# Attention's value products placed one bank behind the transposes, with new spacings for the side work of a two-layer hybrid block

## The chip, the core and the metric

The kernel runs on one core of a Trainium2 chip. A core has a matrix engine, TensorE (PE in the rows, with its weight loads as PEld), and four engines beside it: VectorE (DVE), ScalarE (ACT), GpSimd (POOL) and SyncE (SP), which here issues most of the transfers. Each engine works through a queue of its own in order, and semaphores make one wait for another. The metric is the time of one execution on the device in microseconds (us); less is better.

## What is computed

Two layers, each a feed-forward, a mixer and a second feed-forward, on 256 tokens of width 1024 in float32. Cut to what matters:

```python
for l in range(2):
    x = x + 0.5 * swiglu(rms_norm(x, n1[l]), w1, w2)          # width 2816
    h = rms_norm(x, n2[l])
    u, v, rq, rk, rv, rg, q, kv, gate = split(h @ w_in[l])
    y_a = gelu(u) * (tril(ws) @ layer_norm(gelu(v)) + bs)       # gated mlp, 4 groups
    y_b = silu(rg) * group_norm(retention(rq, rk, rv))          # 4 heads
    y_c = g0 * compressed + g1 * selected + g2 * window         # attention, 8 heads
    ga, gb, gc = split(sigmoid(h @ w_merge[l] + b))
    x = x + (ga*(y_a @ wb[0]) + gb*(y_b @ wb[1]) + gc*(y_c @ wb[2])) @ w_o[l]
    x = x + 0.5 * swiglu(rms_norm(x, n3[l]), w3, w4)
return rms_norm(x, final)
```

At this length the selected and the window branch both see every earlier token, so each of the two is plain causal attention with a bias by distance; the kernel calls them the two `b` of a unit.

## The kernel before

**Weights.** Every weight matrix is cut into pieces of up to 128 x 1024 numbers. `issue` (lines 206 to 228) loads a piece, and splits it into a rounded part (`hi`, a cast on ACT, line 219) and the rest (`lo`, a subtraction on DVE and, for a share set by `pool_lo`, on POOL, line 223). There are four buffers for raw and four for split pieces, and pieces are issued up to three ahead. Activations are split in the same way, so that one product is three matmuls in the fast float32 form (`mm_feat`): high by high, high by low, low by high. Almost all matmuls go through the helper `mm` (line 147), all transposes through `transpose` (line 157).

**Order on PE.** The order of PE's instructions is the order of the program; that of the other engines is chosen by a scheduler when the program is built, by a priority that follows the order of the program. `soon()` raises the priority of what stands in it by 120 instructions. The main stream (the feed-forward's and the mixer's large products) is one generator that yields after each three matmuls. Small work with a chain of its own (attention, retention, the gated mlp, the compressed branch, the column and the transposes of a norm) stands in other generators, the sides. A counter `clk` adds an assumed duration for each matmul (0.1095 for a product of 256 columns). A side that yields a number sleeps until the counter has grown by it; one that yields a condition sleeps until an event is set. After each yield of the main stream `run_sides` goes through the sides and lets those go on that are due; what they emit stands in PE's queue at this place. The `WAIT_` constants are these numbers.

**Attention.** `attention` runs four units one after the other: query tile 0 and 1, group 0 and 1 (`unit`). A unit emits scores for four heads, `WAIT_SCORE[qt]` apart, with the softmax on DVE and ACT (lines 642 to 651); before its second head it waits until the unit before has emitted its last transposes. After `WAIT_P` it goes through its banks (two for tile 0, four for tile 1): four transposes of probabilities into a bank of tag `sc`, a split of them into `ph` (ACT, line 680) and `pl` (DVE, line 681, shown as a part of tile `xhl`), then, `WAIT_PT[qt]` later, the two products `pv` with the values into bank `o`. `cmp_branch` (two of them) does the softmax of the compressed branch, transposes it after `WAIT_CB`, multiplies it when both units of the tile are done, adds it, and splits the sum into `yh[2]` and `yl[2]` (lines 725 to 727).

**The other sides.** `retention` ends in two sets of four transposes into a bank each, which ACT reads four times (line 798). `gmlp` is there four times, once a group; all four start when retention's normalised rows and the mlp's layer norm are there, sleep `WAIT_GMLP`, and emit their products into a bank of tag `ms`, which DVE's addition (line 849) empties. PSUM has two banks `mm`, three `sc`, one `o`, two `ms`.

**Norms.** A norm's scale is applied late: `x_update` (line 376) adds a finished tile of 128 features to x, and `norm_tile` makes the next stage's split operand of it (ACT line 311, DVE line 312) and its squares (`square`: POOL lines 327 to 337; the last tile's square on ACT and its sum on DVE). The side `norm_end` sleeps, emits two short float32 products (`norm_col`: the sum over features as a column), sleeps again, and emits two transposes that spread the factor; the next stage's evacuations wait for it, not its products. The mixer's last part, the output projection, has eight such tiles, one piece each; during it splits are shared 5 to 3 between DVE and POOL.

Of the kernel before, what the change touches and what calls it, by code (L numbers as in the profile page):

```python
# [39 lines left out]
WAIT_FOLD = 3.0  # L40
WAIT_CMP = 7.0
WAIT_COPY = 0.5
WAIT_SCORE = (5.3, 4.5)
WAIT_PT = (4.5, 2.6)
WAIT_CB = 8.0
WAIT_GN = 3.5
WAIT_OB = 1.5
WAIT_LN = 6.0
WAIT_GMLP = 10.0
WAIT_VR = 3.5  # L50
WAIT_P = (2.5, 4.5, 2.5, 2.5)


def _pieces():
# [11 lines left out]
def tile_hybrid_block(  # L66
# [28 lines left out]
    def nm(s):  # L95
        uid[0] += 1
        return f"{s}_{uid[0]}"
# [34 lines left out]
    def soon():  # L132

        return tc.high_priority(offset=EARLY)
# [21 lines left out]
    def transpose(o, i):  # L156
        nc.tensor.transpose(o, i, ident)  # L157
        clk[0] += 0.109
# [17 lines left out]
    def side(gen):  # L176
        sd = Side(gen)
        sd.kind = gen.__name__
        sides.append(sd)
        return sd  # L180
# [127 lines left out]
    def norm_tile(st, k, late=False):  # L308
        if st["i"] < 6:
            g = g_norm[:, st["i"], k:k + 1]  # L310
            S.activation(st["h"][:, k], xs[k], AF.Copy, scale=g)  # L311
            V.scalar_tensor_tensor(st["l"][:, k], xs[k], g, st["h"][:, k].bitcast(F32), op0=ALU.mult, op1=ALU.subtract)  # L312
        if late:
            return
        square(st, k)
# [58 lines left out]
        return lambda: "R" in st  # L374

    def x_update(d, p, nst):
        V.scalar_tensor_tensor(xs[d], p, 0.5, xs[d], op0=ALU.mult, op1=ALU.add)  # L377
        norm_tile(nst, d)


    def ffn(st, nxt, first=False, load=None):
# [104 lines left out]
    def mixer(l, st, nxt):  # L486
# [126 lines left out]
        def unit(qt, g):  # L613
# [52 lines left out]
            def pv(n):  # L666
                b, kb = banks[n]
                ph, pl = PT.pop(n)
                v2 = VS[:, kb, b, 2 * g:2 * g + 2].rearrange("p c d -> p (c d)")
                mm(o, lhsT=v2, rhs=ph, start=n == 0, stop=False)  # L670
                mm(o, lhsT=v2, rhs=pl, start=False, stop=n == len(banks) - 1)

            for n, (b, kb) in enumerate(banks):
                pt = psc()
                for j in range(4):
                    transpose(pt[:, j * 128:j * 128 + 128], Ps[j][:, b, kb * 128:kb * 128 + 128])
                ph = act.tile([128, 512], F32R, tag="ph", name=nm("ph"), bufs=2)
                pl = PL[n % 2]
                with soon():
                    S.copy(ph, pt)  # L680
                    V.tensor_tensor(out=pl, in0=pt, in1=ph.bitcast(F32), op=ALU.subtract)
                PT[n] = (ph, pl)
                if n == len(banks) - 1:
                    ev.add(f"t{qt}{g}")
                yield WAIT_PT[qt]
                pv(n)

            own, oth = slice(64 * g, 64 * g + 64), slice(64 - 64 * g, 128 - 64 * g)
            t = t2()
# [5 lines left out]
        def cmp_branch(qt):  # L695
            yield has(f"s{qt}0", f"s{qt}1")
            sc = scs[qt]
            s3 = sc.rearrange("p (h n) -> p h n", n=16)
            mx = small(8)
            V.tensor_reduce(out=mx, in_=s3, axis=AX.X, op=ALU.max)  # L700
            V.tensor_tensor(out=s3, in0=s3, in1=mx[:, :, None].to_broadcast([128, 8, 16]), op=ALU.subtract)
            S.activation(sc, sc, AF.Exp)
            yield 2.0
            V.tensor_tensor(out=sc, in0=sc, in1=ccmp[:, 1, qt].rearrange("p j g n -> p (j g n)"), op=ALU.mult)
            sm = small(8)
            V.tensor_reduce(out=sm, in_=s3, axis=AX.X, op=ALU.add)
            V.tensor_scalar(sm, sm, 1e-30, None, op0=ALU.max)
            V.reciprocal(sm, sm)
            V.tensor_tensor(out=sm.rearrange("p (j g) -> p g j", g=2), in0=sm.rearrange("p (j g) -> p g j", g=2),
                            in1=gate[qt][:, :, 0].rearrange("p (g j) -> p g j", g=2), op=ALU.mult)  # L710
            V.tensor_tensor(out=s3, in0=s3, in1=sm[:, :, None].to_broadcast([128, 8, 16]), op=ALU.mult)
            yield WAIT_CB
            p = pms()
            transpose(p[:, 0:128], sc)
            ct = sc
            S.copy(ct, p[:, 0:128])
            yield 3.0
            yield has(f"u{qt}0", f"u{qt}1", "yalloc")
            o, p = os[qt], pms()
            for j in range(4):  # L720
                mm(p[:, j * 128:j * 128 + 128], lhsT=VC[:, j], rhs=ct, start=True, stop=True)
            qs = slice(qt * 128, qt * 128 + 128)
            o3 = o.rearrange("p (j t) -> p j t", j=4)
            with soon():
                V.tensor_tensor(out=o, in0=o, in1=p, op=ALU.add)
                S.copy(yh[2][:, :, qs], o3)  # L726
                V.tensor_tensor(out=yl[2][:, :, qs], in0=o3, in1=yh[2][:, :, qs].bitcast(F32), op=ALU.subtract)
            ev.add(f"yc{qt}")
# [11 lines left out]
        def retention():  # L740
# [47 lines left out]
            for it in range(2):  # L788
                yn = yns[:, it]
                p = pms()  # L790
                y = t2()
                ts_ = slice(it * 128, it * 128 + 128)
                for h in range(4):
                    hs = slice(h * 128, h * 128 + 128)
                    transpose(p[:, hs], yn[:, hs])
                for h in range(4):
                    hs = slice(h * 128, h * 128 + 128)
                    S.activation(y[:, hs], p[:, hs], AF.Identity, scale=gnc[:, 0, h:h + 1], bias=gnc[:, 1, h:h + 1])  # L798
                y3 = y.rearrange("p (h t) -> p h t", h=4)
                V.tensor_tensor(out=y3, in0=y3, in1=sg[:, :, ts_], op=ALU.mult)  # L800
                S.activation(yh[1][:, :, ts_], y3, AF.Copy, scale=0.5)
                V.scalar_tensor_tensor(yl[1][:, :, ts_], y3, 0.5, yh[1][:, :, ts_].bitcast(F32), op0=ALU.mult, op1=ALU.subtract)
# [38 lines left out]

        def gmlp(g, z):
            yield lambda: 0 in yh and "gv" in ev and "yn" in ev
            yield WAIT_GMLP
            q = pms()
            for n in range(2):
                mm(q[:, n * 128:n * 128 + 128], lhsT=vl[n][:, g * 128:g * 128 + 128], rhs=wt[:, g], start=True, stop=True)
            y = t2()
            V.tensor_tensor(out=y[:, 0:256].rearrange("p (n t) -> p n t", n=2), in0=q[:, 0:256].rearrange("p (n t) -> p n t", n=2),
                            in1=bsb[:, g:g + 1].to_broadcast([128, 2, 128]), op=ALU.add)  # L850
            V.scalar_tensor_tensor(y[:, 256:512], y[:, 0:256], 0.5, z, op0=ALU.mult, op1=ALU.mult)
            S.copy(yh[0][:, g], y[:, 256:512])
            V.tensor_tensor(out=yl[0][:, g], in0=y[:, 256:512], in1=yh[0][:, g].bitcast(F32), op=ALU.subtract)
            ev.add(f"ya{g}")
# [209 lines left out]
        for d in range(2, 8):  # L1064
            o = pmm()[:, 0:256]
            yield from mm_feat(o, piece(8, 128), mk, True, True)
            x_update(d, o, nst)
        side(norm_end(nst))
        return nst

    def drive(gen):
# [168 lines left out]
```

## Time and profile before

| | |
|---|---|
| median of 3 runs | 1263.14 us |
| lowest, highest | 1262.05, 1270.24 us |
| the profiled execution | 1267.7 us, its span 1265.6 us |
| TensorE, weight loads | busy 98%, 97% of the span |
| VectorE, ScalarE, GpSimd | busy 71%, 53%, 40% |
| mean granted TensorE clock | 0.989 of full speed |

The profile is of one execution. A busy share is the share of the span in which an engine had an instruction at work; matmuls are pipelined and their ends are modelled. L147 is line 147 of the kernel. The views used below: the page (busy times, and the chain of work that ended last), PE's waits (who waited for whom, how long, how often, the longest), the windows (busy time of each engine in a stretch, with the number of instructions in brackets, and the granted clock as a share of 2.4 GHz), the timeline (start, duration, instruction; in square brackets the idle time before it and what ended it), and the instructions of a line with shortest, median and longest duration. In order of time the stages are: feed-forward 0 to 196 us, mixer to 451, feed-forward to 633, and again feed-forward to 819, mixer to 1076, feed-forward to 1250.

### The profile page before, as it was taken

Reading aid. Unit: us, or ns where it says so; the run is one execution under the profiler, and the core shown is the slowest. Engines: PE = TensorE matmul, PEld = TensorE weight load, DVE = VectorE, ACT = ScalarE, POOL = GpSimd, SP = SyncE. Lnnn points to the kernel's source line nnn. Section 1 sums busy time; section 2 is a strip of 40 time slices with the busy share of each in tenths; the row PEclk is TensorE's granted clock in tenths of the full one; section 3 lists DMA queues with packets and bytes.
Section 4 is the critical chain, followed back from the end, with each engine's and each line's share of the span. In section 5 each row is a group of like instructions: output and inputs, shape, how many; then the busy total and the mean of one; then the engine's idle time right before and its main releaser. Section 6 shows DMA issues by size and latency. Waiting matters only on the chain.

```text
span 1265.6 us, 26068 instructions
## 1 busy us (share of the span) xinstructions
PE 1234.9 (98%) x10432; PEld 1222.6 (97%) x10432; DVE 900.2 (71%) x1436; ACT 666.7 (53%) x1070; POOL 504.1 (40%) x419
## 2 busy tenths in 40 slices
PE   9999999998999999999999999999999999999997
PEld 9999999997998999999999999999899989999997
DVE  6766667789875867776667665687897768677653
ACT  6544445567764544554444444465676545445442
POOL 0444231174554735452215442203645548155322
PEclk9999999999999999999999999999999989999998
DMA  8865556754554566666666655675444435556562
GB/s 279 273 185 189 181 191 197 239 161 132 169 167 125 177 186 195 193 190 194 194 189 187 189 176 188 182 238 187 150 137 165 151 129 163 194 197 191 187 195 80
DMA packets 68969, 230.67 MB, mean 182 GB/s; under 512 B 8816, under 2 KB 11504, under 8 KB 68848
## 3 DMA queue, kind: packets, MB, share of 16 engines
q1 hardware_dynamic: 68256, 227.90, 57.6%
q8 instruction: 82, 1.34, 0.4%
q0 software_dynamic: 448, 1.08, 0.3%
q14 instruction: 39, 0.32, 0.1%
q10 hardware_dynamic: 144, 0.03, 0.0%
HBM read 225.80 MB, written 1.05 MB: 179 GB/s over the span
## 4 chain that ended last, share of the span: by engine, by line
PE 83%; DVE 6%; POOL 4%; ACT 3%; issue 2%; DMA 0%; SPq 0%; POOLq 0%; DVEq 0%; ACTq 0%
PE mm L147 56%; PE sc L147 23%; DVE hl L223 2%; PE ms L147 2%; POOL hl L223 2%; ACT hl L219 1%; POOL sq L333 1%; POOL acc L337 1%; PE o L147 1%; PE sc L157 1%; ACT P L646 0%; ACT t L798 0%; DMA x<-in_x_dram 0%; DVE small L649 0%; DVE P L642 0%
## 5 line engine op out<-in xcount | busy, mean ns | idle before, releaser
L219 ACT CAST hl<-raw 128x1024 fp32r<-128x1024 f32 (+3 forms) x437 | 443.2, 1016 | 336.7 <-PE mm L147 179.3
L223 DVE TENSOR_TENSOR hl<-raw,hl 128x896 fp32r<-128x896 f32 (+6 forms) x437 | 476.8, 1093 | 198.9 <-ACT hl L219 197.9
L147 PE MATMUL mm<-xhl,hl 128*128 128x256 f32 x4440 | 541.2, 280 | 3.1 <-ACT hl L219 1.1
L223 POOL TENSOR_TENSOR hl<-raw,hl 128x128 fp32r<-128x128 f32 (+2 forms) x264 | 362.5, 1375 | 431.7 <-ACT hl L219 402.0
L147 PEld LDWEIGHTS mm<-xhl,hl 128*128 128x128 f32 x4440 | 525.8, 189 | 6.2 <-ACT hl L219 1.7
L147 PE MATMUL mm<-s,hl 128*128 128x256 f32 x2496 | 293.5, 279 | 0.0
L147 PEld LDWEIGHTS mm<-s,hl 128*128 128x128 f32 x2496 | 290.7, 188 | 0.2
L147 PE MATMUL sc<-xhl,hl 128*128 128x256 f32 x2280 | 276.7, 280 | 0.0
L147 PEld LDWEIGHTS sc<-xhl,hl 128*128 128x128 f32 x2280 | 269.8, 189 | 0.0
L399 ACT CAST s<-t 128x256 fp32r<-128x256 f32 x88 | 35.7, 406 | 118.2 <-DVE t L398 118.2
L333 POOL TENSOR_TENSOR sq<-x 128x256 f32<-128x256 f32 x36 | 28.3, 786 | 131.7 <-DVE x L377 131.7
L400 DVE TENSOR_TENSOR s<-t,s 128x256 fp32r<-128x256 f32 x88 | 38.4, 437 | 38.3 <-ACT s L399 38.3
L147 PE MATMUL mm<-hl,xhl 128*128 128x256 f32 (+1 forms) x432 | 59.1, 287 | 0.0
L398 DVE TENSOR_TENSOR t<-t,t 128x256 f32<-128x256 f32 x88 | 55.8, 635 | 0.6 <-ACT t L397 0.5
L147 PEld LDWEIGHTS mm<-hl,xhl 128*128 128x128 f32 x432 | 53.7, 189 | 2.2 <-issue 1.9
L337 POOL TENSOR_TENSOR acc<-acc,sq 128x256 f32<-128x256 f32 x36 | 51.3, 1426 | 2.8
L312 DVE SCALAR_TENSOR_TENSOR xhl<-x,gnorm,xhl 128x256 fp32r<-128x256 f32 x48 | 38.8, 817 | 5.5 <-ACT xhl L311 5.5
L646 ACT ACTIVATE P<-P,small 128x128 f32<-128x128 f32 (+1 forms) x64 | 28.9, 451 | 25.5 <-DVE small L642 24.8
L396 DVE TENSOR_TENSOR t<-sc,R 128x512 f32<-128x512 f32 x44 | 30.4, 691 | 10.8 <-PE sc L147 8.2
L397 ACT ACTIVATE t<-t 128x256 f32<-128x256 f32 x88 | 36.2, 412 | 1.4 <-DVE t L396 0.7
L396 DVE TENSOR_TENSOR t<-mm,R 128x512 f32<-128x512 f32 x41 | 28.3, 691 | 8.5 <-PE mm L147 5.9
L147 PE MATMUL sc<-s,hl 128*128 128x256 f32 x192 | 27.8, 309 | 6.3 <-ACT s L726 5.0
(179 smaller groups left out, 742.2 us busy)
## 6 DMA issues: line engine op xcount, KB each, us to landing
raw<-in_w_dram SPq DMA_DIRECT2D x389, 512.0 KB, 3.8
raw<-in_w_dram SPq DMA_DIRECT2D x32, 384.0 KB, 3.1
raw<-in_w_dram SPq DMA_DIRECT2D x4, 420.0 KB, 3.2
x<-in_x_dram SPq DMA_DIRECT2D x4, 256.0 KB, 4.8
raw<-in_w_dram SPq DMA_DIRECT2D x8, 128.0 KB, 4.6
s<-in_c_alibi_dram SPq DMA_DIRECT2D x2, 512.0 KB, 8.5
lng<-in_lnp_dram SPq DMA_DIRECT2D x2, 512.0 KB, 4.2
ks<-ks POOLq DMA_DIRECT2D x4, 256.0 KB, 4.0
```

The source lines that it names most:

```text
L147: nc.tensor.matmul(o, lhsT=lhsT, rhs=rhs, start=start, stop=stop)
L219: S.copy(hi[:, s_], raw[:, s_])
L223: e.tensor_tensor(out=lo[:, a:b], in0=raw[:, a:b], in1=hi[:, a:b].bitcast(F32), op=ALU.subtract)
L312: V.scalar_tensor_tensor(st["l"][:, k], xs[k], g, st["h"][:, k].bitcast(F32), op0=ALU.mult, op1=ALU.subtract)
L333: (V if last else G).tensor_tensor(out=q, in0=xs[k], in1=xs[k], op=ALU.mult)
L337: (V if last else G).tensor_tensor(out=st["acc"], in0=st["acc"], in1=q, op=ALU.add)
L396: V.tensor_tensor(out=t3, in0=p.rearrange("p (a b) -> p a b", a=2), in1=R2, op=ALU.mult)
L397: S.activation(u[:, 0:256], t[:, 0:256], AF.Silu)
L398: V.tensor_tensor(out=u[:, 256:512], in0=u[:, 0:256], in1=t[:, 256:512], op=ALU.mult)
L399: S.copy(h4[:, j % 4], u[:, 256:512])
L400: V.tensor_tensor(out=l4[:, j % 4], in0=u[:, 256:512], in1=h4[:, j % 4].bitcast(F32), op=ALU.subtract)
L646: S.activation(Pt[:, b, 0:nk], Pt[:, b, 0:nk], AF.Exp, scale=-1.0, bias=mx[:, b:b + 1], accum_out=sm[:, b:b + 1])
```

## The change

Attention: in a unit `pv` of a bank is emitted after the transposes of the next bank, and the last one after a last wait. The spacings change: scores of query tile 1 4.2 for 4.5, `WAIT_PT` 6.0 for 4.5 (tile 0) and 2.0 for 2.6 (tile 1), `WAIT_P` of the last unit 0.5 for 2.5, the compressed branch's transposes 6.0 for 8.0 and its next step 1.5 for 3.0. Gated mlp: group g sleeps 2.5 g longer than group 0, and its addition is `soon`. Retention: the four reads of each bank on ACT are `soon`. All norms: `x_update` with what it calls is `soon`. The norm behind a mixer: the column is emitted 5.0 instead of 3.0 behind the last tile, the transposes 3.0 instead of 1.0 behind the column. No instruction is added or taken away.

```diff
--- before.py
+++ after.py
@@ -40,15 +40,17 @@
 WAIT_FOLD = 3.0
 WAIT_CMP = 7.0
 WAIT_COPY = 0.5
-WAIT_SCORE = (5.3, 4.5)
-WAIT_PT = (4.5, 2.6)
-WAIT_CB = 8.0
+WAIT_SCORE = (5.3, 4.2)
+WAIT_PT = (6.0, 2.0)
+WAIT_CB = 6.0
 WAIT_GN = 3.5
 WAIT_OB = 1.5
 WAIT_LN = 6.0
 WAIT_GMLP = 10.0
+WAIT_GROUP = 2.5
+WAIT_LATE = 5.0
 WAIT_VR = 3.5
-WAIT_P = (2.5, 4.5, 2.5, 2.5)
+WAIT_P = (2.5, 4.5, 2.5, 0.5)
 
 
 def _pieces():
@@ -374,8 +376,9 @@
         return lambda: "R" in st
 
     def x_update(d, p, nst):
-        V.scalar_tensor_tensor(xs[d], p, 0.5, xs[d], op0=ALU.mult, op1=ALU.add)
-        norm_tile(nst, d)
+        with soon():
+            V.scalar_tensor_tensor(xs[d], p, 0.5, xs[d], op0=ALU.mult, op1=ALU.add)
+            norm_tile(nst, d)
 
 
     def ffn(st, nxt, first=False, load=None):
@@ -674,6 +677,8 @@
                 pt = psc()
                 for j in range(4):
                     transpose(pt[:, j * 128:j * 128 + 128], Ps[j][:, b, kb * 128:kb * 128 + 128])
+                if n:
+                    pv(n - 1)
                 ph = act.tile([128, 512], F32R, tag="ph", name=nm("ph"), bufs=2)
                 pl = PL[n % 2]
                 with soon():
@@ -683,7 +688,7 @@
                 if n == len(banks) - 1:
                     ev.add(f"t{qt}{g}")
                 yield WAIT_PT[qt]
-                pv(n)
+            pv(len(banks) - 1)
 
             own, oth = slice(64 * g, 64 * g + 64), slice(64 - 64 * g, 128 - 64 * g)
             t = t2()
@@ -714,7 +719,7 @@
             transpose(p[:, 0:128], sc)
             ct = sc
             S.copy(ct, p[:, 0:128])
-            yield 3.0
+            yield 1.5
             yield has(f"u{qt}0", f"u{qt}1", "yalloc")
             o, p = os[qt], pms()
             for j in range(4):
@@ -793,9 +798,10 @@
                 for h in range(4):
                     hs = slice(h * 128, h * 128 + 128)
                     transpose(p[:, hs], yn[:, hs])
-                for h in range(4):
-                    hs = slice(h * 128, h * 128 + 128)
-                    S.activation(y[:, hs], p[:, hs], AF.Identity, scale=gnc[:, 0, h:h + 1], bias=gnc[:, 1, h:h + 1])
+                with soon():
+                    for h in range(4):
+                        hs = slice(h * 128, h * 128 + 128)
+                        S.activation(y[:, hs], p[:, hs], AF.Identity, scale=gnc[:, 0, h:h + 1], bias=gnc[:, 1, h:h + 1])
                 y3 = y.rearrange("p (h t) -> p h t", h=4)
                 V.tensor_tensor(out=y3, in0=y3, in1=sg[:, :, ts_], op=ALU.mult)
                 S.activation(yh[1][:, :, ts_], y3, AF.Copy, scale=0.5)
@@ -841,13 +847,14 @@
 
         def gmlp(g, z):
             yield lambda: 0 in yh and "gv" in ev and "yn" in ev
-            yield WAIT_GMLP
+            yield WAIT_GMLP + WAIT_GROUP * g
             q = pms()
             for n in range(2):
                 mm(q[:, n * 128:n * 128 + 128], lhsT=vl[n][:, g * 128:g * 128 + 128], rhs=wt[:, g], start=True, stop=True)
             y = t2()
-            V.tensor_tensor(out=y[:, 0:256].rearrange("p (n t) -> p n t", n=2), in0=q[:, 0:256].rearrange("p (n t) -> p n t", n=2),
-                            in1=bsb[:, g:g + 1].to_broadcast([128, 2, 128]), op=ALU.add)
+            with soon():
+                V.tensor_tensor(out=y[:, 0:256].rearrange("p (n t) -> p n t", n=2), in0=q[:, 0:256].rearrange("p (n t) -> p n t", n=2),
+                                in1=bsb[:, g:g + 1].to_broadcast([128, 2, 128]), op=ALU.add)
             V.scalar_tensor_tensor(y[:, 256:512], y[:, 0:256], 0.5, z, op0=ALU.mult, op1=ALU.mult)
             S.copy(yh[0][:, g], y[:, 256:512])
             V.tensor_tensor(out=yl[0][:, g], in0=y[:, 256:512], in1=yh[0][:, g].bitcast(F32), op=ALU.subtract)
@@ -1065,7 +1072,7 @@
             o = pmm()[:, 0:256]
             yield from mm_feat(o, piece(8, 128), mk, True, True)
             x_update(d, o, nst)
-        side(norm_end(nst))
+        side(norm_end(nst, WAIT_LATE, 3.0))
         return nst
 
     def drive(gen):
```

## Rows read from the trace of the kernel before

**Rows 1.** The page: busy time by engine, and shares of the chain that ended last.

```profile
PE 1234.9 (98%) x10432; PEld 1222.6 (97%) x10432; DVE 900.2 (71%) x1436; ACT 666.7 (53%) x1070; POOL 504.1 (40%) x419
...
PE 83%; DVE 6%; POOL 4%; ACT 3%; issue 2%; DMA 0%; SPq 0%; POOLq 0%; DVEq 0%; ACTq 0%
```

**Rows 2.** PE's waits over the span: us in total, times, longest us.

```profile
PE sc L147 <- ACT s L726: 5.0, 2, 2.5
PE ms L147 <- DVE t L849: 4.1, 3, 2.8
PE ms L147 <- DVE acc L337: 3.7, 2, 1.9
PE o L147 <- ACT ph L680: 2.7, 2, 1.4
PE sc L147 <- DVE s L727: 1.3, 2, 0.7
PE o L147 <- DVE xhl L681: 1.2, 2, 0.6
```

**Rows 3.** Windows: us, then busy time (count) of PE, PEld, DVE, ACT, POOL; clock, DMA.

```profile
402.00:406.00 4.00, 4.00 (x23) 4.00 (x22) 0.37 (x1) 0.33 (x1) 0.00 (x0) 0.57 0.27 109
1023.00:1031.00 8.00, 7.35 (x37) 7.15 (x38) 2.20 (x4) 1.05 (x1) 0.97 (x1) 0.57 0.20 66
1077.00:1082.00 5.00, 4.62 (x26) 4.62 (x27) 1.30 (x4) 1.32 (x2) 0.75 (x2) 0.66 0.64 213
280.00:320.00 40.00, 34.33 (x281) 32.81 (x281) 37.49 (x96) 29.49 (x66) 18.18 (x17) 1.00 0.49 143
```

**Rows 4.** Timeline of PE, front of attention and mlp, layer 0.

```profile
294.68 0.51 PE L147 MATMUL o<-xhl 128*128 128x512 f32 x1 [0.63 <-DVE xhl L681]
...
300.58 0.71 PE L147 MATMUL ms<-wt,s 128*128 128x128 f32 x4 [2.76 <-DVE t L849]
...
304.54 1.03 PE L157 MATMUL ms<-sq,s 128*128 128x128 f32 x8
```

**Rows 5.** Timeline of DVE, then of ACT, in the same stretch.

```profile
300.11 0.42 DVE L849 TENSOR_TENSOR t<-ms,bsb 128x256 f32<-128x256 f32 x1
...
306.11 2.90 ACT L798 ACTIVATE t<-ms,gnc 128x128 f32<-128x128 f32 x8
```

**Rows 6.** Timeline of PE, then of DVE, end of attention, layer 0.

```profile
392.51 0.60 PE L157 MATMUL sc<-sq,P 128*128 128x128 f32 x4
...
396.15 1.05 PE L147 MATMUL ms<-scc,s 128*128 128x128 f32 x8
...
401.10 4.49 PE L147 MATMUL sc<-s,hl 128*128 128x256 f32 x23 [0.66 <-DVE s L727]
...
393.82 0.69 DVE L681 TENSOR_TENSOR xhl<-sc,ph 128x512 fp32r<-128x512 f32 x1 [2.09 <-ACT ph L680]
```

**Rows 7.** POOL's lines (shortest/median/longest ns) in 430 to 452 us, then the timeline.

```profile
L223 POOL TENSOR_TENSOR hl<-raw,hl x7: 986/1199/1604, 431.3 to 451.3; 128x384 fp32r<-128x384 f32 x7
...
L333 POOL TENSOR_TENSOR sq<-x x6: 792/1195/1602, 432.9 to 448.9; 128x256 f32<-128x256 f32 x6
...
L337 POOL TENSOR_TENSOR acc<-acc,sq x6: 782/802/1199, 433.7 to 450.6; 128x256 f32<-128x256 f32 x6
...
447.92 1.02 POOL L223 TENSOR_TENSOR hl<-raw,hl 128x384 fp32r<-128x384 f32 x1
...
448.92 1.86 PE L147 MATMUL sc<-xhl,hl 128*128 128x256 f32 x15
```

**Rows 8.** Windows of PE: us, busy time (products), clock, DMA share, GB/s.

```profile
60.00:160.00 100.00, 100.00 (x851) 1.00 0.59 185
460.00:560.00 100.00, 100.00 (x885) 1.00 0.66 197
650.00:750.00 100.00, 100.00 (x851) 1.00 0.63 187
1090.00:1190.00 100.00, 100.00 (x885) 1.00 0.59 192
```

## Prediction

> **What bounds the kernel now.** Read the page first: TensorE (PE) is busy for 98% of the span and is 83% of the chain that ended last [rows 1]. The products are the same before and after the change, so it can only win back time in which PE stands still or runs at half clock. PE's waits come next. Six lines there hold 18.0 us [rows 2]; what else PE idles lies at the start and the end of the run, where nothing is edited, and in waits under 0.5 us. Each of the six comes once in each layer's mixer: the attention product `pv` on its split operands `ph` and `xhl` (2.7 + 1.2 us), the gated mlp on the addition that empties its bank (4.1), the branch output on attention's split result (5.0 + 1.3), the norm's column on `acc` (3.7).
>
> Third, the granted clock. Behind most of these waits PE runs at the lower of its two levels, 1.2 instead of 2.4 GHz. A stretch of length t at mean clock c has lost t(1-c). There are five such stretches; three are alike, from 402, 453 and 917 us, and one of these stands with the two others [rows 3]: three times 4 x 0.43, then 8 x 0.43 and 5 x 0.34, so 3 x 1.7 + 3.4 + 1.7 = 10.2 us. They stand behind the waits for attention's result in both layers (402, 1023), for `acc` in both (453, 1077) and for `ph` in layer 1 (917). What the change can reach is 18.0 + 10.2 = 28 us.
>
> **End of attention** (`WAIT_SCORE`, `WAIT_PT`, `WAIT_P`, `WAIT_CB`, the 1.5, `pv` one bank behind). Side work is put into PE's order by the counter `clk`, looked at after every three products, each worth 0.1095, so in steps of 0.3285. From the last scores of the last unit to its last `pv` the waits were 2.5 and four times 2.6, which is 8 + 4 x 8 = 40 steps; they become 0.5 and four times 2.0, which is 2 + 4 x 7 = 30. A score spacing of 4.5 is 14 steps, 4.2 is 13. Against that the two units of the first query tile get 6.0 for 4.5 per bank, 19 steps for 14, which delays the second unit's scores. Followed unit by unit, counting that side work itself advances `clk`, the third unit's scores end 6 products later than before, the fourth's last scores come 9 products earlier and end 12 earlier, and with the 30 of the tail attention ends 42 products earlier. A product takes 0.113 to 0.1175 us (100 us through 885 or 851, [rows 8]). Today PE is through attention's last product at about 397.0 and needs the split result until 401.1 [rows 6], 4.1 us with 3 products to fill them. With 45 products there are 45 x 0.113 = 5.1 us: no wait. The tighter tail holds: the transposes of 392.51 have their split operand at 394.5 [rows 6], 2.0 us later; the new `pv` comes 21 products and a set of transposes behind, at least 2.4 us. Gain: 5.0 + 1.3 of waits and 1.7 + 3.4 of clock, 11.4 us. Bounds: 11.4, and about 3 if DVE or ACT answer 1.5 us later beyond the margin of 1 us in each layer, since waits of 1.3 to 2.5 us stand before the half-clock stretches (the 2.8 of the mlp in layer 0 stands before none).
>
> **Front of attention and the gated mlp.** In layer 0 PE waits for `pv` until 294.68 [rows 4]. The first unit's second transposes and `pv` move back by 1.5 on the counter, 15 products or 1.7 us, so of 2.0 us some 0.3 to 0.5 stay. The four mlp products now come 2.5 apart instead of together. Today the third waits until 300.58 for the addition that starts at 300.11 [rows 4, 5]; DVE had other work before it. Spread, they let retention's two sets of transposes (now at 304.54, behind all four, [rows 4]) in between: counted out, retention's wait ends one step of three products behind the first mlp product. There are two `ms` banks. The order becomes mlp 0, transposes, transposes, mlp 1: the second transposes wait for mlp 0's addition (0.4 us if DVE is free, 3 us if it is as late as today) and mlp 1 for the four ACT reads of the first transposes (eight take 2.90 us and began 0.5 us behind the last transpose, [rows 4, 5]). `soon` moves both forward in the queues, but DVE is busy for 37.5 of the 40 us from 280 to 320 [rows 3]: it has no room to answer at once. What stays or comes new I put at 2.2 us in each layer, between 0.6 and 4. Removed are 2.7 + 1.2 + 4.1 = 8.0 us and the 1.7 us of half clock in layer 1; kept are 8.0 + 1.7 - 4.4 = 5.3 us, between 0 and 8.5.
>
> **The late norm.** The column product goes from 3.0 to 5.0 on the counter behind the last output tile: 16 steps for 10, 18 products later, 2.0 us. That covers the 1.9 us that it waits per layer, by 0.1 to 0.2. `x_update` under `soon` moves a tile's update, scaled copies, square and sum ahead of weight splits that wait. On POOL this matters: through the whole output projection POOL stands still for hardly a moment. By the medians a split there takes 1.20, a square 1.20, a sum 0.80 us [rows 7], 3.20 a tile, while PE needs 24 products, 2.7 to 2.8. POOL falls behind, and the split that ends at 448.94 is taken by PE at 448.92 [rows 7]: no cover at all. If the last tile's square and sum (2.0 us) go before that split, PE waits 2.0 us there instead. I take it that they don't: tile and split already alternate, and a split is ready before the next tile is finished. Gain: 3.7 - 0.3 of waits and 1.7 + 1.7 of clock, 6.8 us; other bound 0.
>
> At their shortest the three take 0.99 + 0.79 + 0.78 = 2.56 us [rows 7]; at that pace POOL would keep up with PE, either order would do and the 6.8 us would be safe, while at the medians and with the other order they are 0. The Trainium skill (GPSIMD Engine Reference, section 1, Specifications) says that POOL shares its SBUF interfaces with VectorE and contends with DVE instructions that have two SBUF inputs, as the weight splits and scaled copies are. By this rule bringing DVE's share of the update forward can keep POOL at the long durations; the spread of the rows agrees with it, but no row says which neighbour made which instruction long.
>
> **Edits at nothing.** `x_update` in the four feed-forwards: four weight buffers, up to three pieces split ahead, cover it, about 8 us; the update's 0.4 us on DVE and 2.0 on POOL fit. Without that cover each of 32 updates would cost up to 2. The power 3.0 instead of 1.0 behind the column: the first evacuation waits 2 us longer, with five banks to fill at 5.4 us each. Transposes ahead of `pv`: they need a third `sc` bank while scores hold two; it is free once the bank before is split, 2 us after its transposes, the same 2.4 us as above.
>
> **Sum.** 11.4 + 5.3 + 6.8 = 23.5 us. The profiled execution took 1267.7 us (span 1265.6 and 2.1 around it): 1244.2. It lies 4.6 above the median of 1263.14 and inside the runs' 1262.05 to 1270.24. On the median the sum gives 1239.6.
>
> **A term of the other sign.** PE's products run at one of two spacings at full clock: [rows 8] has 100 us of each of the four feed-forwards, with the same instructions: both first ones run at the wider spacing (851), both second ones at the closer (885). The second ones begin behind a norm that PE waited for, the first ones behind one it did not wait for. If the late norm no longer stops PE, they may start at the wider one: 0.0045 us x about 1,500 products = 6.8 us each. In layer 0 I expect the next stage to flip the other way, as the second feed-forward now does to it; layer 1 has no next stage. Both feed-forwards behind an unwaited norm being wide, I count one such stage: 1239.6 + 6.8 = 1246. That is the forecast.
>
> **Rivals.** (a) POOL's order turns against PE: the 6.8 us of the norm are not won. 1253 with the wide stage, 1246 without. For it: no cover at 448.9; against: the alternation. (b) DVE sets the pace of the front: it is 94% busy there, so waits return at the `ms` banks as in the upper bound, 5.3 us are lost: 1251 with the wide stage, 1245 without. (c) The change does not do what it says: the stalls are DVE's and ACT's backlog, and wherever PE's order puts the reader, it waits: only a third of the 23.5 is won, 1255, with the wide stage 1262. Against it: at the end of attention DVE itself idles 2.09 us for ACT, which waits for PE [rows 6]. (d) Slower: the priority puts every update's POOL work (2.0 us) before the split that PE needs next. In the output projection, six tiles a layer without cover, that is up to 6 x 2.0 us, 24 in both layers, against at most 16.7 won elsewhere: 1263.1 + 24 - 16.7 = 1270, and with a wide stage 1277. It decides from a wait of 1.4 us a tile. Against it: POOL's backlog then feeds back into a slower PE, which gives POOL time.
>
> **How the numbers follow.** The forecast's case, all three gains within their bounds and none to two wide stages, 0.50, 1237 to 1252. (a) 0.16, (b) 0.14, (c) 0.12, (d) 0.08. Range 1236 to 1258: it leaves out (d), the upper part of (c) and a little below. A measurement here tells about 1% from no change, so faster means under 1250.5. The first case does that in five of six, (a) and (b) in half: 0.42 + 0.15 + 0.03 of (c) = 0.60. Slower is (d), less its milder part, and bad ends of (c): 0.07. Within 1%: 0.33.
>
> **What would show it.** Right: no wait of PE on `s` of line 726 and 727; the `acc` wait under 0.5 us; no half-clock stretch at the ends of attention and mixer; waits of PE at `ms` of 1 to 3 us around 295 to 300, now of transposes on line 849 and of the mlp on line 798. Wrong: PE waiting for `hl` of POOL just before the second feed-forward, which is (a) or (d); a wait on `s` that stays, which is (c). 100 us with 851 products in the last feed-forward shows the wide stage.

## The result and the profile after

The changed kernel took 1249.32 us (median; 1247.98 to 1250.33), the kernel before on the same chip 1262.60 (1259.04 to 1270.24): ratio 0.9868, 95% interval 0.9828 to 0.9909. The forecast was 1246, range 1236 to 1258. The time fits by luck: one term of the forecast came out with the other sign, a second is not there, and the two errors nearly cancel. The profiled execution took 1249.09 us, with a span of 1247.1 against 1265.6.

The page of the changed kernel, the lines that answer to [rows 1]:

```profile
PE 1225.3 (98%) x10432; PEld 1216.7 (98%) x10432; DVE 894.7 (72%) x1436; ACT 667.2 (53%) x1070; POOL 507.7 (41%) x419
...
PE 89%; DVE 5%; issue 2%; ACT 2%; POOL 1%; DMA 0%; SPq 0%; POOLq 0%; DVEq 0%; ACTq 0%
```

PE's waits in it (total us, times, longest), the answer to [rows 2]:

```profile
PE ms L159 <- DVE t L856: 8.6, 2, 4.3
PE mm L149 <- DVE t L964: 1.8, 2, 1.0
PE ms L159 <- POOL rcol L352: 1.0, 1, 1.0
```

All six waits of [rows 2] are gone. In their place stands one that [rows 2] doesn't have: retention's transposes (L159) wait for the gated mlp's addition (L856, which was L849), 4.3 us in each layer. The wait at `rcol` is at the end of the run, as before.

Windows of PE in both kernels: us, busy time (instructions), granted clock, DMA share, GB/s. In order: the end of attention in layers 0 and 1, the norm in both, the front of attention in both. Before:

```profile
380.00:410.00 30.00, 26.84 (x210) 0.94 0.42 123
1005.00:1035.00 30.00, 26.85 (x198) 0.89 0.35 117
440.00:470.00 30.00, 28.14 (x234) 0.94 0.63 184
1070.00:1100.00 30.00, 28.15 (x234) 0.94 0.58 190
280.00:325.00 45.00, 39.33 (x326) 1.00 0.52 152
898.00:943.00 45.00, 40.99 (x325) 0.96 0.46 149
```

After:

```profile
380.00:410.00 30.00, 30.00 (x256) 1.00 0.52 162
1005.00:1035.00 30.00, 30.00 (x264) 1.00 0.53 175
440.00:470.00 30.00, 30.00 (x266) 1.00 0.68 218
1070.00:1100.00 30.00, 30.00 (x267) 1.00 0.60 198
280.00:325.00 45.00, 39.33 (x312) 0.92 0.48 145
898.00:943.00 45.00, 39.60 (x320) 0.96 0.42 137
```

What a window loses is its idle time plus length times (1 - clock). The ends of attention lost 3.16 + 1.8 + 3.15 + 3.3 = 11.4 us and now lose nothing. The norms lost 1.86 + 1.8 + 1.85 + 1.8 = 7.3 us and now lose nothing. The fronts lost 5.67 + 4.01 + 1.8 = 11.5 us and now lose 5.67 + 5.40 + 3.6 + 1.8 = 16.5, which is 5.0 more: 1.4 of waiting and 3.6 of half clock behind the longer wait of layer 0. This measure takes PE's busy time at its word; counted by when the products start, the fronts lost about 2 us (see the ledger, and the sum further down).

The four stretches of feed-forward in the changed kernel, the answer to [rows 8]:

```profile
60.00:160.00 100.00, 100.00 (x852) 1.00 0.60 185
460.00:560.00 100.00, 100.00 (x885) 1.00 0.64 191
650.00:750.00 100.00, 100.00 (x852) 1.00 0.63 187
1090.00:1190.00 100.00, 100.00 (x885) 1.00 0.59 192
```

No feed-forward changed its spacing, so the forecast's wide stage of 6.8 us is not there.

### The profile page after: what moved, and what is told of

The parts are those of the page before. It is cut to its first block, busy times and chain, and to the rows that moved or that the text cites. A ratio compares the mean times of both kernels' runs of the same rounds, so it can differ in the third digit from the quotient of the medians.

```text
span 1247.1 us, 26063 instructions
## 1 busy us (share of the span) xinstructions
PE 1225.3 (98%) x10432; PEld 1216.7 (98%) x10432; DVE 894.7 (72%) x1436; ACT 667.2 (53%) x1070; POOL 507.7 (41%) x419
## 4 chain that ended last, share of the span: by engine, by line
PE 89%; DVE 5%; issue 2%; ACT 2%; POOL 1%; DMA 0%; SPq 0%; POOLq 0%; DVEq 0%; ACTq 0%
PE mm L149 62%; PE sc L149 23%; PE ms L149 2%; DVE hl L225 2%; ACT hl L221 1%; PE o L149 1%; PE sc L159 1%; DMA x<-in_x_dram 0%; PE ms L159 0%; DVE small L652 0%; DVE s L454 0%; DVE t L452 0%; POOL rs L778 0%; POOL hl L225 0%; DVE s L966 0%
## 5 line engine op out<-in xcount | busy, mean ns | idle before, releaser
L225 DVE TENSOR_TENSOR hl<-raw,hl 128x896 fp32r<-128x896 f32 (+6 forms) x437 | 472.6, 1084 | 207.7 <-ACT hl L221 206.5
L225 POOL TENSOR_TENSOR hl<-raw,hl 128x128 fp32r<-128x128 f32 (+2 forms) x264 | 366.0, 1388 | 435.8 <-ACT hl L221 420.3
L352 POOL TENSOR_TENSOR rcol<-col,mhalf 128x2 f32<-128x2 f32 x7 | 5.8, 834 | 61.5 <-DVE col L350 61.5
```

Of the source, the lines that this page charges most:

```text
L225: e.tensor_tensor(out=lo[:, a:b], in0=raw[:, a:b], in1=hi[:, a:b].bitcast(F32), op=ALU.subtract)
```

## A ledger for the experiments

Unchanged kernels differ by far more than the parts to be told apart: 25 runs of the kernel before beside the first experiments took 1257.68 to 1275.18 us. Counted over all pairs of neighbouring products with 256 columns in a trace, PE starts them some 113.35 or some 117.80 ns apart (means of the pairs under and over 115.5); of about 9,650 pairs in each kernel at full clock, 3,005 to 5,829 were wide. Each wide one costs 4.45 ns, so the count alone moves a span by up to 12.6 us. The last columns take that out: span minus 4.45 ns for each wide pair. "Front" is idle time plus half clock of the windows 280 to 325 and 898 to 943 us, as above. "Front, by starts" compares the same numbered products in both traces, from those that start at 280.1 and 898.0 us in the kernel before to those at 380.0 and 1000.0: how much longer the two stretches became, spacing taken out. "Ratio" is to the kernel before on the same chip.

| kernel | median us | ratio, interval | front: idle + half clock | front, by starts | wide pairs | span less spacing | to before |
|---|---|---|---|---|---|---|---|
| before | 1262.60 | | 9.7 + 1.8 |  | 4366 | 1246.2 | |
| changed | 1249.32 | 0.9868 (0.983-0.991) | 11.1 + 5.4 | +2.1 | 4222 | 1228.3 | -17.9 |
| e6 changed, again | 1244.66 | 0.9852 (0.982-0.988) | 10.7 + 3.6 | +1.4 | 3201 | 1227.4 | -18.8 |
| e2 attention alone | 1257.34 | 0.9940 (0.991-0.997) | 12.5 + 5.4 | +3.6 | 4311 | 1236.3 | -9.9 |
| e3 norm alone | 1257.12 | 0.9934 (0.991-0.996) | 8.0 + 3.6 | -0.1 | 3356 | 1238.8 | -7.4 |
| e4 mlp alone | 1268.94 | 1.0024 (0.999-1.006) | 11.0 + 3.6 | +2.7 | 4568 | 1246.1 | -0.1 |
| e8 attention, norm | 1248.40 | 0.9871 (0.985-0.989) | 11.8 + 7.2 | +3.5 | 3250 | 1232.0 | -14.2 |
| e1 mlp behind | 1243.71 | 0.9845 (0.981-0.988) | 10.0 + 3.6 | +1.9 | 4399 | 1228.8 | -17.4 |
| e5 three splits out | 1236.99 | 0.9785 (0.976-0.981) | 6.2 + 1.8 | -4.7 | 3005 | 1221.6 | -24.6 |
| e7 bank read by ACT | 1245.63 | 0.9844 (0.982-0.987) | 9.4 + 5.4 | +1.1 | 4323 | 1227.6 | -18.6 |
| e9 mlp at 9 | 1249.13 | 0.9888 (0.985-0.992) | 9.2 + 7.2 | +2.0 | 5829 | 1228.7 | -17.5 |
| e10 mlp at 8 | 1254.32 | 0.9905 (0.988-0.993) | 11.8 + 9.9 | +7.8 | 5735 | 1234.2 | -12.0 |
| e11 mlp at 6 | 1252.04 | 0.9890 (0.985-0.993) | 10.3 + 3.6 | +4.3 | 4225 | 1230.4 | -15.8 |
| e12 splits on DVE | 1245.20 | 0.9838 (0.980-0.987) | 8.8 + 3.6 | -1.0 | 4268 | 1226.2 | -20.0 |

The changed kernel and its repeat differ by 0.9 us in the last columns, against 5.4 in their spans, and by 0.7 in the front by starts. Differences under about 1 us are not read from it.

## Experiments

**The same kernel once more (e6).** No edit.

> The changed kernel once more, unchanged. If the spacing of the feed-forward's products (851 or 885 in 100 us) is set by the program, its four windows show 852, 885, 852, 885 again. If it is set anew in each execution (the theory drawn from the parts alone, whose windows differ at 60 to 160 us where no line was changed), other numbers can stand there, and the time moves by 6.8 us for each of these stages. Waits and half-clock stretches should be the same in both cases: 8.6 us behind the mlp's addition.

The first of its four stretches (the others are 885, 851 and 885, against 885, 852 and 885):

```profile
60.00:160.00 100.00, 100.00 (x885) 1.00 0.62 193
```

The first feed-forward ran at 885 where the same program ran at 852 before. Over the run that comes to 1,021 wide pairs fewer, 4.5 of the 5.4 us by which the spans differ. The waits are those of the first run (8.5 and 1.8 us). So the spacing belongs to the execution. It is not the chip's either: e7 ran on the chip of e6, its one edit is in the mixer, and its first feed-forward ran at 852. What sets the spacing at its start is open.

**The parts alone (e2, e3, e4) and without the mlp's (e8).** Each takes the other parts' lines back; the mlp's part holds `soon` for retention's reads too. e3 for instance leaves this, and the priority on `x_update` (cut here):

```diff
-        side(norm_end(nst))
+        side(norm_end(nst, WAIT_LATE, 3.0))
```

> The kernel before with the attention part of the change alone (products one bank behind the transposes, the new spacings, the 1.5 before the last transposes' products); the mlp's spread and priorities and the norm's delay are left as before. If the parts are separate, as in my sum: the end of attention gives its 11.4 us (waits 6.3, half clock 5.1), the front keeps the mlp's waits of before (8.0) and loses or keeps the one of 1.7: 1250 to 1253 us, ratio to the kernel before 0.990 to 0.993. If the end of attention is only freed together with the norm or the mlp: no more than 4 us, 1258 or over.

> The kernel before with the norm's part alone (the norm's end 5.0 later with its weight of 3.0, the residual's update with priority). By my sum: the wait on acc (3.4 us) and the half clock behind it (3.4 us) go, 6.8 us, so 1256 us, ratio 0.9946. Rival: the half clock there came out of what precedes it, and only the wait goes: 1259 us, ratio 0.9975. Second rival: feed-forward products with the wide spacing behind it, +6.8, no change.

> The kernel before with the gated mlp's part alone (products 2.5 apart, its addition and ScalarE's reads of the transposes with priority). Theory A (the mlp's place between retention's transposes makes the stall): the waits of 2.8 and 1.2 us per layer behind the mlp's addition go, a stall of some 4 us and half clock behind it come in their place, so 1261 to 1266 us, ratio 0.999 to 1.004. If the stall needs the moved products of attention as well: 1255 to 1258 us, ratio 0.994 to 0.996.

> The changed kernel with the gated mlp's part undone (four products together, no priority for its addition and for ScalarE's reads of the transposes); attention's and the norm's parts stay. By the sum of the parts as measured alone (mlp_only against before no difference): the same as the changed kernel, 1247 to 1252 us, waits of 4.9 us per layer behind the addition in place of 4.3. If the spread is worth what the forecast gave it beside the other parts: 4 to 8 us slower than the changed kernel. If the spread costs what the new place of the transposes suggests: 4 us faster.

With the spacing taken out the parts alone give 9.9, 7.4 and 0.1 us, together 17.4, against 17.9 to 18.8 for the whole. The norm's part alone is worth its forecast (6.8). That the sum comes so near is partly chance: attention and norm together (e8) give 14.2, not 9.9 + 7.4. In e2 PE still waits 3.7 us at the column, but the granted clock of both norm windows is 1.00: the 3.4 us of half clock behind the column went with either part alone, and can be won only once. (In e4, with the same wait, it is there in layer 0 and not in layer 1.) PE's waits in the kernel with attention's part alone:

```profile
PE ms L149 <- DVE t L853: 9.8, 2, 4.9
PE ms L149 <- DVE acc L339: 3.7, 2, 1.9
PE mm L149 <- DVE t L961: 1.9, 2, 1.0
PE sc L149 <- DVE s L731: 1.3, 2, 0.6
```

Of the 6.3 us on `s` the 5.0 on ScalarE's half are gone; the 1.3 on VectorE's stay until the mlp's part joins (e8 has them too, the changed kernel not). And the front is already worse here than in the changed kernel, 17.9 against 16.5 us, with the mlp's four products still together: attention's part alone makes the loss in the front. The mlp's part alone makes one too (e4: 14.6 us against 11.5, 2.7 by starts), gets as much back elsewhere and is worth nothing; beside the other two it is worth 3.7 to 4.6 us (e8 against the changed kernel and its repeat).

**Is it the place between retention's transposes? (e1)** All four mlp products go behind both sets.

```diff
-WAIT_GMLP = 10.0
+WAIT_GMLP = 14.0
```

> One number of the changed kernel: WAIT_GMLP 14.0 in place of 10.0, so that all four products of the gated mlp come on TensorE behind both of retention's groups of transposes and not one of them between. Theory A (the loss at the front of attention comes from the place: the mlp's first product takes the bank that the second transposes need, and they wait for its addition): the two waits of 4.3 us behind the addition go, and with them the half-clock time behind them (0.33 of 10 us in layer 0, 0.12 and 0.05 of 10 us in layer 1). That is 8.6 + 5.0 = 13.6 us at most, so 1236 to 1241 us, ratio to the changed kernel about 0.990 to 0.994. Theory B (VectorE is some 4 us behind with its queue at that point, and whatever reads a bank there next waits as long): the wait moves to another transpose or product, 1247 to 1251 us. Theory C (the mlp's outputs then come late to the mixers' products): a new wait on them after 310 us, over 1251 us.

PE's waits:

```profile
PE ms L149 <- ACT t L804: 3.9, 2, 2.0
PE mm L149 <- DVE s L860: 2.0, 3, 0.7
PE mm L149 <- DVE t L964: 1.6, 2, 0.8
PE mm L149 <- ACT s L859: 1.5, 2, 1.1
```

The 8.6 us are gone and 3.9 + 2.0 + 1.5 have come elsewhere; the front idles 10.0 instead of 11.1 us and the span without spacing is the same (-17.4). The median of 1243.71 looks like a gain of 5.6, but that is another chip, and 0.9845 stands against 0.9868 and 0.9852. Theory A falls. C is in it: 3.5 us are now waits for the mlp's outputs.

**What VectorE does in those 4.3 us.** DVE in the changed kernel:

```profile
294.48 0.83 DVE L225 TENSOR_TENSOR hl<-raw,hl 128x640 fp32r<-128x640 f32 x1
295.23 1.50 DVE L966 SCALAR_TENSOR_TENSOR s<-t,t 128x512 f32<-128x512 f32 x1
296.65 1.61 DVE L225 TENSOR_TENSOR hl<-raw,hl 128x640 fp32r<-128x640 f32 x1
298.19 0.68 DVE L964 TENSOR_TENSOR t<-mm,R 128x512 f32<-128x512 f32 x1
298.79 1.01 DVE L225 TENSOR_TENSOR hl<-raw,hl 128x640 fp32r<-128x640 f32 x1
299.72 0.68 DVE L966 SCALAR_TENSOR_TENSOR s<-t,t 128x512 f32<-128x512 f32 x1
300.33 0.68 DVE L686 TENSOR_TENSOR xhl<-sc,ph 128x512 fp32r<-128x512 f32 x1
300.93 0.41 DVE L856 TENSOR_TENSOR t<-ms,bsb 128x256 f32<-128x256 f32 x1
```

Three weight splits (L225), the gate's three operations (L966, L964, L966) and attention's own split (L686) stand in an unbroken row ahead of the addition, whose operand PE had finished by 296.04. In the kernel before the third split came behind the mlp's additions, and in e2 it stands ahead of them:

```profile
305.06 0.81 DVE L223 TENSOR_TENSOR hl<-raw,hl 128x640 fp32r<-128x640 f32 x1
```

```profile
299.19 1.01 DVE L225 TENSOR_TENSOR hl<-raw,hl 128x640 fp32r<-128x640 f32 x1
...
301.33 0.74 DVE L853 TENSOR_TENSOR t<-ms,bsb 128x256 f32<-128x256 f32 x2
```

**Take the splits away (e5).** Three low halves per layer are left out, VectorE's share and GpSimd's; the products that used them take the high half twice, so PE's work is the same and the values are not.

```diff
-                if a < b:
+                if a < b and len(queue) not in NO_LOW:
```

> The changed kernel without the low halves of three weight pieces per layer (104 to 106 and 319 to 321 of the list, the ones split at 294 to 300 us): their subtractions on VectorE and GpSimd are left out, and TensorE's products take the high half twice, so its work is the same and the values are not. Theory A (the mlp's place between retention's transposes is the cause): the waits of 4.3 us stay above 3. Theory B (VectorE's pile of splits stands in front of the mlp's addition: 0.83 + 1.61 + 1.01 us of them, and 0.8 us that the product beside them takes longer): the addition comes some 3 to 4 us earlier, the two waits fall to 0.3 to 1.5 us each and the half-clock time at 300 to 310 us goes. That is 6 to 8 us of waits and up to 5 of clock: 1237 to 1243 us, ratio to the changed kernel 0.990 to 0.995.

Its waits, then DVE in the same place (8 us earlier by the spacing and the gain):

```profile
PE ms L172 <- DVE t L873: 4.0, 2, 2.0
```

```profile
289.18 0.69 DVE L983 SCALAR_TENSOR_TENSOR s<-t,t 128x512 f32<-128x512 f32 x1 [0.60 <-ACT t L982]
289.79 0.68 DVE L981 TENSOR_TENSOR t<-mm,R 128x512 f32<-128x512 f32 x1
291.60 0.69 DVE L983 SCALAR_TENSOR_TENSOR s<-t,t 128x512 f32<-128x512 f32 x1 [1.12 <-ACT t L982]
292.21 0.68 DVE L703 TENSOR_TENSOR xhl<-sc,ph 128x512 fp32r<-128x512 f32 x1
292.81 0.41 DVE L873 TENSOR_TENSOR t<-ms,bsb 128x256 f32<-128x256 f32 x1
```

The wait is halved, 8.6 to 4.0 us, and the front loses 8.0 instead of 14.3 to 16.5; by starts it is 4.7 us shorter than in the kernel before. Without spacing the span is 5.8 to 6.7 us shorter than in the changed kernel. The rest stays above the expected 0.3 to 1.5 each: the addition still stands behind the gate's second operation, which waits 1.12 us for ScalarE's tanh while VectorE has nothing else it may take. Theory B holds, with that second link.

**Free the bank by another engine (e7).** A copy on ScalarE reads the bank.

```diff
+                S.copy(y[:, 0:256], q[:, 0:256])
```

> The changed kernel with the gated mlp's bank read by a copy on ScalarE, which stood idle for 2.0 us there, and the addition made on VectorE out of the copy: one instruction of 0.4 us more on ScalarE for each mlp product, VectorE's work the same. Theory B (the bank is held only because VectorE's queue is late): the second transposes no longer wait for the addition, their wait falls from 4.3 to 0.5 to 1.5 us, and the half-clock time behind it goes; 1240 to 1245 us, ratio to the changed kernel 0.992 to 0.997. Rival (the front is paced by VectorE's sum of work, whatever bank is free): the wait comes back at the next thing that VectorE owes, the sum of waits at 290 to 325 us stays at 5 to 6 us; 1247 to 1251 us.

ACT in it:

```profile
299.53 0.63 ACT L966 ACTIVATE t<-t 128x512 f32<-128x512 f32 x1 [2.02 <-DVE t L965]
300.06 0.57 ACT L685 CAST ph<-sc 128x512 fp32r<-128x512 f32 x1
300.53 0.38 ACT L856 COPY t<-ms 128x256 f32<-128x256 f32 x1
```

ScalarE's idle 2.0 us are no room: it stands at the tanh, which waits for VectorE's L965, and the copy is behind that in the queue. The wait falls only from 4.3 to 3.2 us, the span without spacing by at most 0.7. VectorE's lateness reaches PE through either reader.

**Move the addition up in VectorE's order (e9, e10, e11).** WAIT_GMLP 9, 8 and 6.

```diff
-WAIT_GMLP = 10.0
+WAIT_GMLP = 9.0
```

> WAIT_GMLP 9.0 in place of 10.0 in the changed kernel. The mlp's first product comes 3 products earlier, and in VectorE's order its addition stands ahead of the third split (1.01 us), of the gate's product L966 (0.68) and of attention's subtraction L686 (0.68); retention's transposes keep their place. Theory B (what stands in front of the addition on VectorE makes the wait): the wait of 4.3 us falls by the 2.4 us of these three, to some 2 us per layer, and may go to a reader behind them; 1240 to 1246 us, front 3 to 6 us shorter than in the changed kernel. If VectorE's whole work paces the front: the same sum of waits at 290 to 325 us, at another line.

> WAIT_GMLP 8.0. The mlp's first product stands ahead of attention's transposes, its addition on VectorE ahead of the second L964 and the third split, its second product ahead of retention's transposes, which come 12 products later. Theory B: the addition is made right behind the second split, some 3 us earlier than in the changed kernel, and no transpose waits for it; what is left is the second product's addition, 1 to 2 us. 1238 to 1245 us. Pace theory (VectorE's sum): 1245 to 1250 us.

> WAIT_GMLP 6.0. Two of the mlp's products stand ahead of attention's transposes and their additions ahead of the second L964 and the third split; that work is now in front of the gate's additions L964 (0.68 us), whose bank TensorE needs. Theory B: no transpose waits for the mlp, but the wait at L964, 1.8 us in all in the changed kernel, grows by the 1.2 us per layer of the two additions and their products: waits of 3 to 5 us in the front over both layers instead of 10; 1238 to 1244 us. Pace theory: 1245 to 1250 us.

PE in e9, the two places of layer 0:

```profile
299.83 0.66 PE L159 MATMUL ms<-sq,s 128*128 128x128 f32 x4 [2.13 <-DVE t L856]
302.04 1.22 PE L149 MATMUL ms<-wt,s 128*128 128x128 f32 x4 [1.55 <-ACT t L804]
```

The addition came 2 us earlier and its wait fell to 2.1 us as expected, but the next product waits 1.55 for ScalarE's reads of the transposes. The front idles 9.2, 11.8 and 10.3 us against 10.7 to 11.1, and by starts it is 2.0, 7.8 and 4.3 us longer than before, against 1.4 to 2.1: no order wins, and e10, which splits its wait into three (1.1, 2.4 and 1.7 us in layer 0), loses 9.9 us to half clock and 6 us of span. My expectation of 3 to 6 us from the order alone fell. The waits come back at other lines, as the pace theory has it; its times of 1245 to 1250 us were passed by e10 (1254.32) and e11 (1252.04).

**Splits without GpSimd beside them (e12).** The three pieces are split by VectorE alone.

```diff
-            cut = m if cuts > 1 else (kn * pool_lo[0] // 8) * n
+            cut = m if cuts > 1 or len(queue) in WHOLE else (kn * pool_lo[0] // 8) * n
```

> The changed kernel with the three weight pieces of the front of each layer split by VectorE alone (1024 columns instead of 640, GpSimd none). By the length of 0.83 us for 640 columns without GpSimd beside it, one takes some 1.3 us, three 3.9 us against the 3.45 us of today. If GpSimd's work beside VectorE's is what makes a split 1.61 and L966 1.50 us long (0.83 and 0.68 alone): L966 falls to 0.68, all three splits take 1.3 us each, and the addition comes 0.4 us earlier, and by L966's later place another 0.7: wait 3.0 to 3.5 us in place of 4.3. If they are long for another reason: splits of 2 us and more, the addition 1.5 us later, wait over 5 us. Time 1243 to 1250 us in both cases.

DVE in it:

```profile
295.11 1.23 DVE L226 TENSOR_TENSOR hl<-raw,hl 128x1024 fp32r<-128x1024 f32 x1
296.25 0.69 DVE L967 SCALAR_TENSOR_TENSOR s<-t,t 128x512 f32<-128x512 f32 x1
296.85 1.22 DVE L226 TENSOR_TENSOR hl<-raw,hl 128x1024 fp32r<-128x1024 f32 x1
...
298.58 1.22 DVE L226 TENSOR_TENSOR hl<-raw,hl 128x1024 fp32r<-128x1024 f32 x1
```

VectorE does 60% more columns in each split, and all three take 3.67 us against 3.45; the gate's operation takes 0.69 instead of 1.50. The wait falls to 3.2 us, as expected if GpSimd's work made them long; the front loses 12.3 us, the span without spacing is 1.2 to 2.1 shorter than in the changed kernel. Its ratio of 0.9838 is the lowest of the complete kernels here, but its interval (0.980 to 0.987) overlaps that of the changed one.

## Why the prediction was right in time and wrong in two steps

**End of attention: right.** No wait on `s` and no half clock are left: the windows give 11.4 us, the start times 12.3, the forecast was 11.4. By e2 and e8, 1.3 of it needs the mlp's part.

**Late norm: right, for the delay alone.** The windows give 7.3, the start times 7.2, the part alone 7.4, the forecast 6.8. The margin is thinner than the 0.1 to 0.2 us expected. PE, then DVE, at the column of layer 0 in the changed kernel:

```profile
448.07 0.27 PE L149 MATMUL ms<-ones,acc 128*128 128x1 f32 x1
```

```profile
446.80 1.22 DVE L339 TENSOR_TENSOR acc<-acc,sq 128x256 f32<-128x256 f32 x1 [0.63 <-POOL acc L339]
```

The last sum ends at 448.02 and PE takes it at 448.07. GpSimd's tiles and splits alternate as before. The priority on `x_update` was not run by itself. In e3, which has it, GpSimd's order of instructions is that of the kernel before, and VectorE's and ScalarE's differ only within 20 us behind the late norms; so rivals (a) and (d) had nothing to stand on, and no wait for `hl` of GpSimd is seen.

**Front of attention and mlp: wrong, a gain of 5.3 forecast, a loss found: 5.0 by idle time and half clock, 2.1 by start times.** The failed step is the term "what stays or comes new", put at 2.2 us in each layer between 0.6 and 4. It was 4.3 + 0.9 = 5.2, and half clock of 3.6 us came behind it in layer 0 where none was counted. The 1.7 us of half clock in layer 1, counted as removed, stayed. The step had the right wait in the right order, but it bounded the addition's lateness by today's 3 us. It is later than today, because attention's new order lets the third split and the gate's second pair pass ahead of it on VectorE (e2 has this without the mlp's edit). The removed 8.0 us were real.

**Rival (b): the mechanism that happened**, at 0.14, with its time of 1245 to 1251. VectorE sets the pace: taking work from it helps (e5), moving the reader or the bank does not (e1, e7, e9 to e11). About half of the wait outlives the splits (e5, 4.0 of 8.6 us); there VectorE itself waits 1.12 us for ScalarE's tanh. What (c) says of the whole change is wrong at the end of attention and right in the front.

**Wide stage: wrong, 6.8 us that are not there.** The last feed-forward ran at 885 behind a norm that nobody waited for, and the first at 852 and 885 in one and the same program (e6). The spacing was read as a consequence of what precedes the stage; it is a draw of the execution. It put the forecast 6.8 us too high, and the front put it 7.4 too low (5.3 us won in the forecast, 2.1 lost by start times): that the time fits is luck.

**The sum.** The span fell by 18.5 us, of which 0.6 is spacing; the windows find 11.4 + 7.3 - 5.0 = 13.7 where 23.5 had been forecast. Counted instead by the start times of numbered products in both traces (all 9,792 of the fast form with 256 columns come in the same number, spacing taken out), the ends of attention (380.0 to 440.0 and 1000.0 to 1065.1 us in the kernel before) give 5.9 + 6.5 = 12.3 us, the norms behind them 3.6 each, and the fronts lose 1.8 + 0.3 = 2.1: 17.4, nearly the whole. So most of what the windows miss is in the fronts, where they show PE busier in the kernel before than its progress bears out. A product that stands alone is busy for 0.28 us, one in a row follows 0.113 us behind the last, so interrupted stretches look busier than they are, and the fronts were interrupted more often before (by 12 waits of over 0.15 us, now by 7). Whether that is all of the difference is not shown.

## What to carry to other kernels

Here the new wait's releaser was busy for 90% of the stage (35.85 of the 40 us from 280 to 320 in the changed kernel), and a new place for the reader moved the wait and did not remove it. In such a case take work from that engine, and read its queue ahead of the instruction, not its mean. A bound taken from "as late as today" is not a bound when the change also reorders what stands in front. Before a term of a few microseconds is drawn from a difference between stages, look whether a second execution of the same program shows it.

## What was not expected of the hardware

GpSimd's help cost VectorE more than it gave: three splits of 640 columns took 3.45 us and the first L966 0.81 more than in e12, together 4.26, against 3.67 for three splits of all 1024 columns (e12). In the changed kernel a split of 640 columns took 0.83 us when it started ahead of GpSimd's and 1.61 behind it, and L966, with both operands in SBUF, 1.50 instead of 0.69; L964, with one operand in PSUM, took 0.68 in either case. The Trainium skill (SBUF — State Buffer, "SBUF: two separate sides") says that a VectorE operation with two SBUF inputs and a GpSimd one that reads SBUF exclude each other for a whole instruction; e12 agrees, with 0.69 and three times 1.22 us once GpSimd has no part.

The half clock behind the same wait varies. Behind 4.3 us in layer 0 the windows lost 3.6 us in one execution of the changed kernel and 1.8 in the next, and e10's three shorter waits in a row lost 5.0 in each layer.

Equal products ran 113.35 or 117.80 ns apart at full granted clock, one of the two through nearly the whole of a feed-forward and mixed in the mixers, and which one was drawn anew in each execution.
